# Seven products in place of eight: three more weight pairs of an up projection, with two more buffers and a longer lead

## The chip, the core and the metric

The kernel runs on one core of a Trainium2 chip. The metric is device time in microseconds (us). A core has a matrix engine (PE), whose weight loads are listed apart as PEld; a vector engine (DVE); a scalar engine (ACT); GpSimd (POOL); and SyncE (SP), which here issues most of the DMAs. Each engine works through its own instructions in order and waits on semaphores for the others.

## The reference: what is computed

One decoder layer on 256 tokens of width 2048, in float32: an input projection, two kinds of attention heads, an output projection, a gated MLP and a gate at the end. The change lies in the first product of the MLP, the up projection (`D_FF` is 5632):

```python
h = rms_norm(x, ffn_norm_g[i])
u = h @ w_up[i]                       # (256, 2048) @ (2048, 11264)
a, g = jnp.split(u, 2, axis=-1)
a = causal_dwconv(a, conv_w[i], conv_b[i])
x = x + (jax.nn.gelu(a, approximate=False) * g) @ w_down[i]
```

## The kernel before

**Split numbers.** A float32 product is made of three matrix passes in float32r. Every operand is split into `hi` (the value rounded to float32r) and `lo` (what is left), and a block product is `ah*hi + ah*lo + al*hi` (function `three`, lines 368 to 370). For the weights the split is done on the core, after a load of 512 KB has landed in a "raw" buffer: ACT casts raw to `hi` (line 1308), DVE subtracts `hi` from raw (line 1311). Both halves of a split fill one buffer of 128x1024 each.

**Column groups.** The up projection goes by eleven column groups, `q` = 0 to 10. A group takes 512 columns of `a` and the 512 of `g` that belong to them, for all 256 tokens, and sums over 16 chunks of 128 rows of the weight (k). A plain unit is one k: 2 token halves x 2 column halves = 4 block products, 12 matmuls of 128x512. Its four sums (`up00` to `up11`) fill four of the eight PSUM banks.

**Sevens.** Two k's together make a product of 2x2 blocks by 2x2 blocks, which has eight block products. `seven(r)` does it with seven (the scheme of Strassen and Winograd): sums of weight blocks on DVE, sums of token blocks made beforehand (`S_up`), and seven block products. It is made of four units, which have one, two, two and two block products. They also need one split of 128x512 and three of 128x1024, where two plain units need two of 128x1024, and four additions of 128x512 on DVE (lines 1736 to 1739). Four products (`upP1`, `upP5`, `upP6`, `upP7`) gather over all sevens of a group in the other four PSUM banks. At the last seven of a group they are combined into `z_up` (lines 1765 to 1768), which is added to the group's result afterwards. The table `ORDERS` says for each group where plain units (`p`) and the units of its sevens (`a`, `b`, `c`, `d`) stand. Before the change the groups 0 to 10 have 2, 0, 4, 0, 4, 1, 2, 1, 2, 1 and 1 sevens: 18.

**What else DVE and ACT do for a group.** When the last unit of a group is through, ACT moves the four sums to `EZ` (line 1158, four instructions), and DVE adds `z_up` (line 1165, two instructions) and transposes in blocks (line 205, two). DMAs of POOL and SP turn the result (line 211). Some units later ACT and DVE make the convolution, the GELU, the product with `g` and its split (lines 1184 to 1197, 161, 162), and for the down projection the sums of line 473 to 477. All of this is hooked to fixed units of the next group.

**Lead and buffers.** `run_units` writes the program unit by unit. Before unit `i` it loads as far ahead as raw buffers are free, and splits units up to `i + ahead - 1` as far as split buffers are free. `AHEAD_UP` is 4; in the stretch with four sevens it is 6. There are eight split buffers (`hi0` to `hi3`, `lo0` to `lo3`), and four more (`y0` to `y3`, in the tile `uB`, which is filled with results only later) from the seventh unit of group 1 to the eighth of group 5. Raw buffers are `raw0` to `raw2`, `v4`, and `v0` to `v3`, of which two go two units into group 9 and two go two units into group 10. A seven holds its two raw buffers from its first unit's load to its last unit's split. The order on each engine is then set by a list scheduler when the program is built, so that matmuls of neighbouring units stand mixed on PE.

Of the kernel before, what the change touches and what calls it, by code (L numbers as in the profile page):

```python
# [33 lines left out]

BLK = 1024
RAW, PARTS = 3, 4
AHEAD_UP, AHEAD_FOUR, AHEAD_LATE = 4, 6, 6

SEVEN = (2, 4, 6, 8, 10, 12, 14, 16, 18)
FIRST = (0, 1, 2, 3, 5, 7, 4, 9, 6, 11, 8, 13, 10, 15, 12, 17, 14, 19, 16, 20, 18, 21)  # L40
# [6 lines left out]
UP_K = (4, 5, 6, 7, 0, 1, 2, 3, 8, 9, 10, 11, 12, 13, 14, 15)  # L47
NONE, ONE, TWO = "p" * 16, "pppppp" "apapapap" "pppp", "ppp" "apapapap" "bpbpbpb" "pp"
FOUR = "p" "aapaap" "bbpbb" "ccpccp" "ddpdd" "p"
ORDERS = ("pppppp" "apapapap" "bpbbbp", NONE, FOUR, NONE, FOUR, ONE, TWO, ONE, TWO, ONE, ONE)  # L50
START = [sum(map(len, ORDERS[:q])) for q in range(12)]
TURN_AT = (-1, -1, 0, 0)
GATE_LAST = "ppp" "apapapap" "bbbb" "ppppp"
# [9 lines left out]
def layer_kernel(  # L63
# [29 lines left out]
    def f32(ap):  # L93
        return ap.bitcast(F32)
# [413 lines left out]
    with mixers:  # L508
# [51 lines left out]
        def evac(dst, c0, n, func=AF.Copy):  # L560
            def f(t, b):
                act.activation(dst()[:, t, c0 : c0 + n], b[:, :n], func, scale=r1["t"][:, t : t + 1])
            return f

        def get(name):
            def f():
                if name not in z:
                    z[name] = zbuf(name)
                return z[name]
            return f  # L570
# [320 lines left out]
        def mv_evac(grp):  # L891
            def f(t, b):
                if "mv" not in z:
                    z["mv"] = zbuf("mv")
                    ov = z["mv"].rearrange("p t (h c) -> p t h c", h=MH)[:, :, :, 256:257]
                    pool.memset(ov, 1.0)
                dst = z["mv"][:, t, grp * 516 : (grp + 1) * 516].rearrange("p (h c) -> p h c", h=2)
                act.activation(dst[:, :, 0:256], b.rearrange("p (h c) -> p h c", h=2), AF.Copy,
                               scale=r1["t"][:, t : t + 1])
            return f  # L900
# [38 lines left out]
        def with_after(b, hook):  # L939
            fn = b.fn  # L940
            b.fn = lambda hi, lo: (fn(hi, lo), hook())
# [52 lines left out]
        for c in range(2):  # L994
            f = mv_evac(c)
            add(C_MV + c * 512, 512, after(f, mlstm_out) if c == 1 else f)
        for c in range(2):
            f = evac(get("mo"), c * 512, 512, AF.Sigmoid)
# [96 lines left out]
    with tc.tile_pool(name="ffn", bufs=1) as fp:  # L1095
# [4 lines left out]
        uB = fp.tile([P, 8, 512], F32R, tag="uB", name="uB")  # L1100
        uC = fp.tile([P, 8, 512], F32R, tag="uC", name="uC")
# [58 lines left out]
        def up_turn(with_z):  # L1160

            y = Y.rearrange("p (t b c) -> p t b c", t=NT, b=4)

            def summed(t):
                return lambda: dve.scalar_tensor_tensor(
                    out=EZ[:, t], in0=xs[:, 1, t * BLK : (t + 1) * BLK], scalar=r2["t"][:, t : t + 1], in1=EZ[:, t],
                    op0=ALU.mult, op1=ALU.add)

            def turned(t):
                def f():  # L1170
                    square(y, t, 0, EZ[:, t])
                    if t == NT - 1:
                        with tc.issue_after(last["load"]):
                            move(y, Z, nc.sync)
                return f
            return [f(t) if f is turned or with_z else (lambda: None) for t in range(NT) for f in (summed, turned)]
# [33 lines left out]

        late = {}
        now = [0]
        spaces = [f"raw{i}" for i in range(RAW)] + [f"{k}{i}" for k in ("hi", "lo") for i in range(PARTS)] + ["v0", "v1", "v2", "v3", "v4", "y0", "y1", "y2", "y3"]
        until = {"v0": 8, "v1": 8, "v2": 9, "v3": 9}
        splits = (*spaces[RAW : RAW + 2 * PARTS], "y0", "y1", "y2", "y3", "w0", "w1", "w2", "w3")
        held, used = set(), {}
        for j in range(done[0] - PARTS, done[0]):
            used[f"hi{j % PARTS}"] = used[f"lo{j % PARTS}"] = used[f"raw{j % RAW}"] = len(used)
# [1 line left out]
        def free_spaces(j):  # L1220

            def may(t):
                if t in until:
                    return 7 <= j < START[until[t] + 1] + 2
                if t[0] == "y":
                    return START[1] + 6 <= j < START[5] + 8
                if t == "v4":
                    return j >= 26 and (not late or j < late["x"])
                if t[0] == "x":
                    return j < late["x"]  # L1230
                return (t not in ("pT", "ring") or j < late["gate"]) and (t != "pT" or now[0] > late["x"] - 8) and (t != "pT" or now[0] > late["x"] - 8) and (t not in ("e0", "e1", "ring") or now[0] > late["free"])

            return sorted((t for t in spaces if t not in held and may(t)), key=lambda t: used.get(t, -1))

        def free_of(j, kind):

            return [t for t in free_spaces(j) if (t in splits) == kind]

        def space(j, name, kind):
            tag = free_of(j, kind)[0]  # L1240
            held.add(tag)
            i = int(tag[-1]) if tag[-1].isdigit() else 0
            if tag == "ring":
                v = ring[:, 0:2].rearrange("p a b -> p (a b)")
            elif tag[0] == "e":
                v = EZ[:, i]
            elif tag == "v4":
                v = xs[:, 0, BLK : 2 * BLK]
            elif tag[0] == "y":
                v = f32(uB[:, 2 * i : 2 * i + 2]).rearrange("p k c -> p (k c)")  # L1250
            elif tag[0] == "v":
                v = spare_raws[f"u{32 + 4 * (i // 2)}"][:, i % 2]
            elif tag[0] == "x":
                v = xs[:, 1, i * BLK : (i + 1) * BLK]
            elif tag[0] == "w":
                v = f32(late["w"][:, i]) if i < 4 else late["w2"][:, i - 4]
            elif tag == "pT":
                v = fp.tile([P, BLK], F32R if kind else F32, tag=tag, name=name)
                v = f32(v[:]) if kind else v
            else:  # L1260
                v = wp.tile([P, BLK], F32R if kind else F32, tag=tag, name=name, bufs=1)
                v = f32(v[:]) if kind else v
            return tag, v

        def give(tags):
            for t in tags:
                held.remove(t)
                used[t] = max(used.values(), default=0) + 1
# [48 lines left out]
        def run_units(us, first_late, gate):  # L1317
            loaded = split = 0
            for i, u in enumerate(us):
                if i == first_late:  # L1320
                    v = apool.tile([P, 4, BLK], F32R, tag="aT0", name="w2", bufs=2)
                    S2 = apool.tile([P, 2, BLK], F32R, tag="aT1", name="S2", bufs=2)
                    v2 = apool.tile([P, 2, BLK], F32, tag="aT2", name="w2b", bufs=2)
                    spaces.extend(("w0", "w1", "w2", "w3", "w4", "w5", "pT", "e0", "e1", "ring", "x0", "x1"))
                    late.update(gate=gate, x=i + 20, free=i + 26, w=v, w2=v2, S=S2.rearrange("p b (i c) -> p b i c", c=256))
                ahead = AHEAD_LATE if i >= first_late else AHEAD_FOUR if START[1] + 4 <= i < START[5] else AHEAD_UP
                now[0] = i
                while True:
                    if loaded < len(us) and len(free_of(loaded, False)) >= len(us[loaded].srcs):
                        us[loaded].load(loaded)  # L1330
                        loaded += 1
                    elif split < min(loaded, i + ahead) and len(free_of(split, True)) >= us[split].needs:
                        us[split].split(split)
                        split += 1
                    else:
                        break
                u.fn(*u.parts)
                give(u.holds)
# [350 lines left out]
        def between(hook):  # L1689
            def f():  # L1690
                with tc.issue_after(last["hi"]), tc.issue_after(last["lo"]), tc.issue_after(last["load"]):
                    hook()
            return f
# [5 lines left out]
        def up_group(q):  # L1699
# [3 lines left out]

            n7 = len(set(ORDERS[q]) - {"p"})
            first = 2 * n7
# [83 lines left out]
            kinds = {"p": iter(us), **{c: iter(seven(r)) for r, c in enumerate("abcd"[:n7])}}  # L1789
            return [next(kinds[c]) for c in ORDERS[q]]  # L1790

# [14 lines left out]
        first_late = len(us)  # L1806
# [20 lines left out]
        for q in range(KF // 4):  # L1827
            for job, i in zip(up_turn("a" in ORDERS[q]), TURN_AT if q < KF // 4 - 1 else (-1, 0, -1, 1)):
                with_after(us[START[q + 1] + i], between(job))
            for i, job in enumerate(up_act(q)):  # L1830
                if q < KF // 4 - 1:
                    at = ACT_AT.get(len(ORDERS[q + 1]), ACT_ELSE)
                    with_after(us[START[q + 1] + at[i]], between(job))
# [35 lines left out]
```

## Time and profile before

| what | value |
|---|---|
| median of 3 runs | 1227.51 us (1227.32 to 1229.55) |
| the profiled execution's own time | 1227.41 us |
| its span, first to last instruction | 1225.7 us |
| PE busy | 1219.0 us (99%) |
| DVE busy | 1026.9 us (84%) |
| ACT busy | 765.5 us (62%) |
| POOL busy | 178.7 us (15%) |
| DMA engines, mean busy share by queue | 65.4% and 5.0% for the two large ones |
| granted PE clock | 1.00 |

The busy share of PE is made of matmuls that overlap (one is listed with 0.39 us, while the next starts earlier), so it says that PE always has work, not how long a matmul costs. For that the distance from start to start is read. A wait of an engine is listed with what ended it. The up projection fills the stretch from about 425 us to 898 us of the span.

### The profile page before, as it was taken

The page shows a single profiled execution, that of the slowest core. Times are in us where ns is not written, and L with a number is a line of the kernel's source. Part 1 is how long each engine was busy: PE and PEld are TensorE (multiplying, and loading weights), DVE is VectorE, ACT ScalarE, POOL GpSimd, SP SyncE. Part 2 cuts the span into 40 slices and gives each one's busy share as a digit, 9 for nine tenths or more (in the row PEclk, how much of TensorE's full clock was granted, in tenths as well). Part 3 has the DMA queues.
Part 4 walks back from the last instruction along what each step waited for, and adds up shares of the span by engine and source line. Part 5 has one row for each costly group of instructions (what it writes and reads, how often), then busy time and mean ns, then how long its engine had stood idle before and what let it go on. Part 6 is the DMA issues. An engine that isn't in the chain of part 4 may idle for free.

```text
span 1225.7 us, 16382 instructions
## 1 busy us (share of the span) xinstructions
PE 1219.0 (99%) x5541; PEld 1025.6 (84%) x5541; DVE 1026.9 (84%) x1299; ACT 765.5 (62%) x1119; POOL 178.7 (15%) x331
## 2 busy tenths in 40 slices
PE   9999999999999999999999999999999999999998
PEld 7999988888888888888888888888888888888887
DVE  6788767675679989898898998898788999999796
ACT  8567545565655666776686676767657555556653
POOL 2011237243301401101101100110110000050000
PEclk9999999999999999999999999999999999999999
DMA  8566587676565796767677687756797895785652
GB/s 308 184 193 195 165 241 221 184 216 195 165 234 177 236 292 206 250 215 246 225 264 221 188 267 252 222 175 223 236 315 244 305 359 206 266 252 209 198 200 69
DMA packets 126964, 276.36 MB, mean 225 GB/s; under 512 B 14793, under 2 KB 26817, under 8 KB 126881
## 3 DMA queue, kind: packets, MB, share of 16 engines
q1 hardware_dynamic: 115344, 257.27, 65.4%
q0 software_dynamic: 11008, 17.76, 5.0%
q8 instruction: 43, 0.70, 0.2%
q10 hardware_dynamic: 529, 0.30, 0.1%
q14 instruction: 40, 0.33, 0.1%
HBM read 247.99 MB, written 8.93 MB: 210 GB/s over the span
## 4 chain that ended last, share of the span: by engine, by line
PE 99%; DMA 0%; DVE 0%; SPq 0%; ACT 0%; issue 0%; DVEq 0%
PE up L368 11%; PE up L370 11%; PE up L369 11%; PE tg L357 6%; PE tg L358 6%; PE tg L359 6%; PE pg L368 5%; PE pg L369 5%; PE pg L370 5%; PE gt L370 2%; PE gt L369 2%; PE gt L368 2%; PE upP L368 1%; PE upP L370 1%; PE upP L369 1%; PE dnP L1361 1%
## 5 line engine op out<-in xcount | busy, mean ns | idle before, releaser
L369 PE MATMUL up<-part,x2T 128*128 128x512 f32 x523 | 203.5, 389 | 0.0
L370 PE MATMUL up<-part,x2T 128*128 128x512 f32 x524 | 203.4, 390 | 0.0
L303 DVE TENSOR_TENSOR lo<-raw,hi 128x1024 fp32r<-128x1024 f32 (+3 forms) x119 | 139.2, 1171 | 76.1 <-ACT hi L301 75.7
L1308 ACT CAST part<-raw 128x1024 fp32r<-128x1024 f32 (+1 forms) x139 | 138.7, 1007 | 98.2 <-PE up L370 21.4
L1311 DVE TENSOR_TENSOR part<-raw,part 128x1024 fp32r<-128x1024 f32 (+1 forms) x135 | 155.6, 1162 | 31.6 <-ACT part L1308 27.2
L301 ACT CAST hi<-raw 128x1024 fp32r<-128x1024 f32 (+3 forms) x119 | 120.1, 1011 | 96.3 <-PE tg L359 43.3
L368 PE MATMUL up<-part,x2T 128*128 128x512 f32 x524 | 167.2, 389 | 0.0
L368 PEld LDWEIGHTS up<-part,x2T 128*128 128x128 f32 x524 | 98.4, 188 | 20.3
L369 PEld LDWEIGHTS up<-part,x2T 128*128 128x128 f32 x523 | 98.2, 188 | 20.5
L370 PEld LDWEIGHTS up<-part,x2T 128*128 128x128 f32 x524 | 98.2, 188 | 20.2
L359 PE MATMUL tg<-hi,hT 128*128 128x512 f32 x288 | 113.6, 395 | 0.0
L358 PE MATMUL tg<-lo,hT 128*128 128x512 f32 x288 | 113.3, 393 | 0.0
L357 PE MATMUL tg<-hi,hT 128*128 128x512 f32 x288 | 112.4, 396 | 0.0
L211 POOL DMA_DIRECT2D EZ<-Y x66 | 35.0, 538 | 279.6 <-issue 122.1
L359 PEld LDWEIGHTS tg<-hi,hT 128*128 128x128 f32 x288 | 54.1, 188 | 11.0
L358 PEld LDWEIGHTS tg<-lo,hT 128*128 128x128 f32 x288 | 54.1, 188 | 10.9
L357 PEld LDWEIGHTS tg<-hi,hT 128*128 128x128 f32 x288 | 53.8, 188 | 10.6
L1308 ACT CAST part<-u36r 128x1024 fp32r<-128x1024 f32 x41 | 43.0, 1050 | 21.5 <-PE up L370 15.9
L369 PE MATMUL pg<-lo,hT 128*128 128x430 f32 (+1 forms) x156 | 55.7, 357 | 0.0
L370 PE MATMUL pg<-hi,hT 128*128 128x430 f32 (+1 forms) x156 | 55.5, 356 | 0.0
L1311 DVE TENSOR_TENSOR part<-u36r,part 128x1024 fp32r<-128x1024 f32 x39 | 47.4, 1217 | 6.4 <-ACT part L1308 5.6
L1308 ACT CAST part<-u32r 128x1024 fp32r<-128x1024 f32 (+1 forms) x35 | 34.5, 990 | 24.6 <-PE up L370 8.0
(984 smaller groups left out, 2949.0 us busy)
## 6 DMA issues: line engine op xcount, KB each, us to landing
raw<-in_w_up_dram SPq DMA_DIRECT2D x77, 512.0 KB, 4.9
raw<-in_w_in_dram SPq DMA_DIRECT2D x71, 512.0 KB, 4.4
raw<-in_w_down_dram SPq DMA_DIRECT2D x42, 512.0 KB, 5.5
u36r<-in_w_up_dram SPq DMA_DIRECT2D x41, 512.0 KB, 5.3
u32r<-in_w_up_dram SPq DMA_DIRECT2D x36, 512.0 KB, 5.2
xs<-in_w_up_dram SPq DMA_DIRECT2D x22, 512.0 KB, 5.1
w2b<-in_w_down_dram SPq DMA_DIRECT2D x20, 512.0 KB, 5.6
raw<-in_w_out_dram SPq DMA_DIRECT2D x17, 512.0 KB, 4.8
```

The source lines that it names most:

```text
L211: (other if other and (4 * a + b) % 3 else pool).dma_start(out=c[32 * b : 32 * b + 32, a::4], in_=y[32 * a : 32 * a + 32, :, b])
L301: act.copy(hi, raw)
L303: dve.tensor_sub(lo, raw, f32(hi))
L357: pe.matmul(o, ah, hi[:, i, :], start=first, stop=False)
L358: pe.matmul(o, ah, lo[:, i, :], start=False, stop=False)
L359: pe.matmul(o, al, hi[:, i, :], start=False, stop=last)
L368: pe.matmul(o, ah, hi, start=start, stop=False)
L369: pe.matmul(o, ah, lo, start=False, stop=False)
L370: pe.matmul(o, al, hi, start=False, stop=stop)
L1308: act.copy(r32(hi), raw)
L1311: dve.tensor_sub(r32(lo), raw, hi)
L1361: pe.matmul(o, al, hi, start=False, stop=last)
```

## The change

Groups 5, 7 and 9 get two sevens in place of one, so that groups 5 to 9 have two each, 21 sevens in all. Two split buffers `y4` and `y5` are added in the upper half of the tile `uC`. They may be used from the seventh unit of group 1 to the eighth unit of group 8. While units of groups 5 to 7 are in turn, units up to `i + 4` are split ahead, in place of `i + 3`.

```diff
-AHEAD_UP, AHEAD_FOUR, AHEAD_LATE = 4, 6, 6
+AHEAD_UP, AHEAD_TWO, AHEAD_FOUR, AHEAD_LATE = 4, 5, 6, 6
...
 NONE, ONE, TWO = "p" * 16, "pppppp" "apapapap" "pppp", "ppp" "apapapap" "bpbpbpb" "pp"
 FOUR = "p" "aapaap" "bbpbb" "ccpccp" "ddpdd" "p"
-ORDERS = ("pppppp" "apapapap" "bpbbbp", NONE, FOUR, NONE, FOUR, ONE, TWO, ONE, TWO, ONE, ONE)
+ORDERS = ("pppppp" "apapapap" "bpbbbp", NONE, FOUR, NONE, FOUR, TWO, TWO, TWO, TWO, TWO, ONE)
...
-        spaces = [... "v4", "y0", "y1", "y2", "y3"]
+        spaces = [... "v4", "y0", "y1", "y2", "y3", "y4", "y5"]
...
                 if t[0] == "y":
-                    return START[1] + 6 <= j < START[5] + 8
+                    return START[1] + 6 <= j < START[5 if t < "y4" else 8] + 8
...
-                v = f32(uB[:, 2 * i : 2 * i + 2]).rearrange("p k c -> p (k c)")
+                v = f32(uB[:, 2 * i : 2 * i + 2] if i < 4 else uC[:, 2 * i - 4 : 2 * i - 2]).rearrange("p k c -> p (k c)")
...
-                ahead = AHEAD_LATE if i >= first_late else AHEAD_FOUR if START[1] + 4 <= i < START[5] else AHEAD_UP
+                ahead = AHEAD_LATE if i >= first_late else AHEAD_FOUR if START[1] + 4 <= i < START[5] else AHEAD_TWO if START[5] <= i < START[8] else AHEAD_UP
```

The built program changes in three places that matter for what follows. The first is on DVE, in group 1, where the two new buffers come into use (`part` is a split buffer, the first operand behind the arrow is raw, the second `hi`):

```order
-L1311 TENSOR_TENSOR part_1_4620<-raw_0_4473,part_0_4619 128x1024
+L1311 TENSOR_TENSOR uC<-raw_0_4473,uC 128x1024
 L473 TENSOR_TENSOR Sd_up<-Sd_up 128x2x128
-L1311 TENSOR_TENSOR part_1_4626<-raw_0_4485,part_0_4625 128x1024
-L1311 TENSOR_TENSOR part_1_4642<-u36r,part_0_4641 128x1024
+L1311 TENSOR_TENSOR part_1_4624<-raw_0_4485,part_0_4623 128x1024
+L1311 TENSOR_TENSOR part_1_4640<-u36r,part_0_4639 128x1024
```

The same work stands in the same order there; only its buffers differ.

The second place is on DVE, where group 9 opens. Before, with one seven in that group, which comes later, the stretch around the additions and transposes for group 8 reads:

```order
L1311 TENSOR_TENSOR part_1_7288<-raw_0_7175,part_0_7287 128x1024
L475 TENSOR_TENSOR Sf<-xs,Sf 128x128
L1165 SCALAR_TENSOR_TENSOR EZ<-xs,rstd_ffn,EZ 128x1024 x2
L477 TENSOR_TENSOR Sp<-Sf,Sp 128x4x128
L205 STREAM_TRANSPOSE Y<-EZ 128x8x4x32 x2
L1311 TENSOR_TENSOR part_1_7328<-raw_0_7194,part_0_7327 128x1024
```

Now, with the first seven already in the fourth unit:

```order
L1311 TENSOR_TENSOR part_0_7264<-xs,part_0_7264 128x512
L475 TENSOR_TENSOR Sf<-xs,Sf 128x128
L1165 SCALAR_TENSOR_TENSOR EZ<-xs,rstd_ffn,EZ 128x1024 x2
L1736 TENSOR_TENSOR xs<-xs 128x512
L477 TENSOR_TENSOR Sp<-Sf,Sp 128x4x128
L205 STREAM_TRANSPOSE Y<-EZ 128x8x4x32 x2
L1311 TENSOR_TENSOR part_1_7302<-raw_0_7171,part_0_7301 128x1024
```

What stands ahead of the stretch is now a half split (128x512), and one addition of the seven stands within it.

The third place is the same spot on PE. Before, from the last use of the split ahead of that stretch to the first use of the one behind it:

```order
L369 MATMUL up_7296<-part_1_7288,x2T_3876 128x512
L370 MATMUL up_7296<-part_0_7287,x2T_3876 128x512
L368 MATMUL up_7293<-part_0_7327,x2T_3876 128x512
L368 MATMUL up_7295<-part_0_7327,x2T_3876 128x512
L368 MATMUL up_7294<-part_0_7327,x2T_3876 128x512
L368 MATMUL up_7296<-part_0_7327,x2T_3876 128x512
L368 MATMUL upP_7420<-part_0_7362,x2T_3876 128x512
L369 MATMUL up_7293<-part_1_7328,x2T_3876 128x512
```

Now:

```order
L369 MATMUL upP_7344<-part_0_7264,x2T_3876 128x512
L370 MATMUL upP_7344<-part_0_7264,x2T_3876 128x512
L368 MATMUL up_7270<-part_0_7301,x2T_3876 128x512
L369 MATMUL up_7267<-part_1_7302,x2T_3876 128x512
```

The first use of the low part behind the stretch stood 53 matmuls behind the last matmul of group 8, and stands 43 behind it now. From the middle of group 10 to the end of the program the instructions of PE, DVE and ACT stand in the same order as before.

More of the change, by code (lines that the diff above doesn't have):

```diff
@@ L1212, in layer_kernel @@
         now = [0]
-        spaces = [f"raw{i}" for i in range(RAW)] + [f"{k}{i}" for k in ("hi", "lo") for i in range(PARTS)] + ["v0", "v1", "v2", "v3", "v4", "y0", "y1", "y2", "y3"]
+        spaces = [f"raw{i}" for i in range(RAW)] + [f"{k}{i}" for k in ("hi", "lo") for i in range(PARTS)] + ["v0", "v1", "v2", "v3", "v4", "y0", "y1", "y2", "y3", "y4", "y5"]
         until = {"v0": 8, "v1": 8, "v2": 9, "v3": 9}
-        splits = (*spaces[RAW : RAW + 2 * PARTS], "y0", "y1", "y2", "y3", "w0", "w1", "w2", "w3")
+        splits = (*spaces[RAW : RAW + 2 * PARTS], "y0", "y1", "y2", "y3", "y4", "y5", "w0", "w1", "w2", "w3")
         held, used = set(), {}
```

## The prediction

> **What bounds the kernel now.** I read the page first, then PE's waits, then the stretches of groups 5 to 10.
>
> ```profile
> span 1225.7 us, 16382 instructions
> PE 1219.0 (99%) x5541; PEld 1025.6 (84%) x5541; DVE 1026.9 (84%) x1299; ACT 765.5 (62%) x1119; POOL 178.7 (15%) x331
> PE 99%; DMA 0%; DVE 0%; SPq 0%; ACT 0%; issue 0%; DVEq 0%
> PE warm L111 <- DVE ones L107: 1.1, 1, 1.1
> PE xT L173 <- DMA xs<-in_x_dram: 0.5, 1, 0.5
> ```
>
> The chain that ended last is PE for 99%, and PE's only two waits, the last two rows, are at the program's start. So each matmul taken away shortens the run by one matmul's time, as long as PE still never waits. The price of a matmul is its distance from start to start:
>
> ```profile
> 442.22 0.39 PE L368 MATMUL up<-part,x2T 128*128 128x512 f32 x1
> ...
> 444.94 0.39 PE L369 MATMUL up<-part,x2T 128*128 128x512 f32 x1
> ```
>
> Thirteen starts, twelve steps, 2.72 us: 0.2267 us a step, though each row says 0.39. The other engine near its limit is DVE. Here groups 5 to 10 stand in stretches (us, PE, PEld, DVE, ACT, POOL, granted clock, DMA):
>
> ```profile
> 642.00:682.00 40.00, 40.00 (x178) 33.15 (x177) 34.81 (x37) 24.73 (x36) 3.77 (x7) 1.00 0.73 231
> 682.00:724.00 42.00, 42.00 (x186) 34.68 (x186) 38.80 (x43) 30.65 (x43) 3.75 (x7) 1.00 0.73 230
> 724.00:766.50 42.50, 42.50 (x189) 35.19 (x188) 36.93 (x38) 27.52 (x38) 3.77 (x7) 1.00 0.76 238
> 766.50:809.00 42.50, 42.50 (x189) 35.19 (x188) 39.35 (x44) 30.61 (x42) 3.75 (x7) 1.00 0.66 209
> 809.00:851.50 42.50, 42.50 (x189) 35.19 (x188) 36.83 (x38) 27.51 (x38) 3.77 (x7) 1.00 0.69 216
> 851.50:898.00 46.50, 46.50 (x207) 38.51 (x206) 37.75 (x39) 29.84 (x40) 3.73 (x7) 1.00 0.77 242
> ```
>
> Groups with two sevens (second and fourth row) load DVE with 38.80 and 39.35, those with one (third, fifth) with 36.93 and 36.83. DVE keeps up, but not evenly. Where a group opens it must do the additions and transposes for the group before, and meanwhile makes no weight splits. How near that comes is the lead: the time from the end of a split to PE's first use of its low part. Matching the order of the program with the trace, the opening of group 6 has the smallest:
>
> ```profile
> 694.94 1.22 DVE L1311 TENSOR_TENSOR part<-raw,part 128x1024 fp32r<-128x1024 f32 x1
> 696.33 0.40 PE L369 MATMUL up<-part,x2T 128*128 128x512 f32 x1
> ```
>
> The split ends at 696.16, PE wants it at 696.33: 0.17 us to spare.
>
> **The change, part by part.** *Removed.* A pair of plain units has 8 block products, a seven has 7: 3 matmuls less, for three sevens 9. The built program has 9 fewer. 9 x 0.2267 = 2.04 us.
>
> [...]
>
> *Added.* For each seven ACT and DVE split 3 x 1024 + 512 in place of 2 x 1024 columns, and DVE adds four times.
>
> ```profile
> L1311 DVE TENSOR_TENSOR part<-raw,part 128x1024 fp32r<-128x1024 f32 x38 | 46.2, 1217 | 9.4 <-ACT part L1308 9.2 <-issue 0.2
> L1311 DVE TENSOR_TENSOR part<-u32r,part 128x512 fp32r<-128x512 f32 x3 | 2.1, 686 | 0.4 <-ACT part L1308 0.4
> L1736 DVE TENSOR_TENSOR u32r<-u32r 128x512 f32<-128x512 f32 x3 | 2.0, 672 | 0.0
> L1308 ACT CAST part<-raw 128x1024 fp32r<-128x1024 f32 x37 | 38.8, 1051 | 22.4 <-PE up L370 9.0 <-DVE raw L1737 4.4 <-PE up L369 3.7
> ```
>
> DVE: 1.22 + 0.69 + 4 x 0.67 = 4.6 us a seven; neighbours overlap by about 0.08, so six instructions cost about 4.1. By the stretches a second seven has cost 39.35 - 36.88 = 2.5. A group with two sevens is 186 matmuls on PE, 42.2 us; DVE in it is between the measured 39.35 and 36.88 + 4.1 = 41.0. On average it is hidden behind PE, with 1.2 to 2.8 us to spare in a group. ACT gains some 1.7 us on 27.5: hidden. Loads are the same bytes: nothing on SP or in the DMA queues but their order.
>
> *The openings of groups 6, 7 and 8.* They get one unit more of lead, which on PE is 9 to 12 matmuls, 2.0 to 2.7 us, and two buffers to hold it. From 0.17 that is 2 us and more: no wait, price nothing. Without that cover group 6 would wait for about what its opening adds.
>
> *The opening of group 9.* Here the lead is back at three units and the two buffers are gone, but a second seven has come in. This spot is in the trace, with one seven:
>
> ```profile
> 808.31 2.43 ACT L1158 ACTIVATE EZ<-up,rstd_ffn 128x512 f32<-128x512 f32 x4 [0.53 <-PE up L370]
> 811.81 1.21 DVE L1311 TENSOR_TENSOR part<-raw,part 128x1024 fp32r<-128x1024 f32 x1
> 812.94 0.28 DVE L475 TENSOR_TENSOR Sf<-xs,Sf 128x128 f32<-128x128 f32 x1
> 813.14 2.47 DVE L1165 SCALAR_TENSOR_TENSOR EZ<-xs,rstd_ffn,EZ 128x1024 f32<-128x1024 f32 x2
> 815.53 0.68 DVE L477 TENSOR_TENSOR Sp<-Sf,Sp 128x512 fp32r<-128x512 f32 x1
> 816.14 2.36 DVE L205 STREAM_TRANSPOSE Y<-EZ 128x1024 f32<-128x1024 f32 x2
> 818.43 1.18 DVE L1311 TENSOR_TENSOR part<-raw,part 128x1024 fp32r<-128x1024 f32 x1
> ...
> 821.25 0.39 PE L369 MATMUL up<-part,x2T 128*128 128x512 f32 x1
> ```
>
> The split behind the stretch ends at 819.61, PE uses it at 821.25: 1.64 to spare. In the new order the split ahead is a half one (start to start about 0.60 in place of 1.13) and one addition comes in (about 0.60): the end moves to 819.68. PE's first use moves from 53 to 43 matmuls behind the end of group 8, as the order shows, mostly because a seven's first unit holds PE for 3 matmuls and not 12: 821.25 - 10 x 0.2267 = 818.98. So the split is late by 0.70 us, and PE waits so long. What is queued behind that matmul is all of group 9, so the wait goes to the end in full, once; DVE is then ahead again.
>
> Bounds of this wait. Below: nothing, if ACT and DVE come 0.7 earlier (ACT waits for PE's last sums in the first row above). Above: the half split that opened group 8,
>
> ```profile
> 769.69 0.68 DVE L1311 TENSOR_TENSOR part<-raw,part 128x512 fp32r<-128x512 f32 x1
> 775.47 0.39 PE L369 MATMUL upP<-part,x2T 128*128 128x512 f32 x1
> ```
>
> had a lead of 5.10; with the stretch of 7.25 on DVE (0.20 + 2.39 + 0.61 + 2.29 from the starts above, 0.60 for the addition, 1.16 for the split) and 3 matmuls on PE, 5.10 + 0.68 - 7.25 = -1.47. I take 0.70, from the rows of the spot itself.
>
> *Sum.* -2.04 + 0.70 = -1.34 us. The profiled execution took 1227.41 and would take 1226.07; the median of the runs is 0.10 above it, so 1226.2. The gain is 0.11%; a measurement of this kernel can tell about 0.2% (2.46 us) from no change, and the full 2.04 us would also stay below that.
>
> **The rivals.** *No wait at all.* Group 9 opens in time and the whole 2.04 is kept: 1225.5. For it: PE has not waited once at eleven openings, and the scheduler mixes matmuls of several units. Against it: 0.17 and 1.64 us are little room.
>
> *DVE becomes the bound, slower.* DVE waits too:
>
> ```profile
> DVE part L1311 <- ACT part L1308: 18.9, 21, 2.1
> ACT part L1308 <- PE up L370: 32.1, 25, 5.7
> ```
>
> That is 18.9 us in the 220 us of groups 5 to 9, 3.7 a group. If these waits stay while the work grows, groups 5, 7 and 9 need 41.0 + 3.7 = 44.7 on DVE against 42.2 on PE, 2.5 us too much each. The first of it is taken from the room at the openings (1.64 and the 2.0 to 2.7 of the new unit, about 4), the rest PE waits: 3 x 2.5 - 4 = 3.5, and 1227.51 - 2.04 + 3.5 = 1229.0. It decides from the point where a group costs DVE over 42.2 with its waits. Against it: the second row says that ACT itself waits for PE to free a buffer, so these waits are slack, and more buffers shorten them.
>
> *Late loads.* In group 10, with few raw buffers, ACT waited for a load:
>
> ```profile
> 874.84 2.00 ACT L1308 CAST part<-raw 128x1024 fp32r<-128x1024 f32 x2 [4.27 <-DMA raw<-in_w_up_dram]
> ```
>
> PE did not. Group 9 now has a second seven that holds two of the six raw buffers left. A wait of this size on the lead of 1.64 would cost 2.6: 1226.2 + 2.6 = 1228.8. Against it: counting units in the program, loads there still stand 7 or more units ahead of use, over 14 us.
>
> [...]
>
> **How the numbers follow.** The forecast with a wait of 0.3 to 1.5 us has 0.50 (1225.8 to 1227.0), no wait 0.25, DVE as the bound 0.14, late loads 0.08, something else 0.03. Range: 1225.2, a little under the full gain, to 1228.2, which takes in the mild part of the two slow rivals: about 0.8. Faster by over 0.2%, under 1225.05, needs more than the matmuls give: 0.08. Slower by over 0.2%, above 1229.96, is the bad part of the slow rivals: 0.07. The rest, 0.85, is within 0.2%.
>
> **What would show it.** In the profile after: 9 matmuls fewer (some records may be missing); in groups 5 to 9 steps of 0.2267 with no gap except one of about 0.7 us at the fourth unit of group 9, where PE waits for DVE's line 1311; DVE at 39 to 41 us in each of these groups; leads at the openings of groups 6 to 8 of 2 us or more. Gaps at several openings, or DVE idle for ACT as much as before while PE waits, would make the prediction wrong, as would a load that PE's wait goes back to.

## The result, and the profile after

The changed kernel takes 1244.47 us (median; 1242.42 to 1246.9). Beside it the kernel before took 1227.51 again. The ratio is 1.0136, with a 95% interval of 1.0124 to 1.0147: slower by 17 us, where 1226.2 was forecast with a range up to 1228.2. The profiled execution of the changed kernel is the longest of its five (1246.9).

The page of the changed kernel, with the lines that answer to those of before:

```profile
span 1245.2 us, 16395 instructions
PE 1224.9 (98%) x5532; PEld 1026.8 (82%) x5532; DVE 1039.2 (83%) x1317; ACT 769.8 (62%) x1125; POOL 179.2 (14%) x331
PE 95%; DMA 1%; DVE 1%; SPq 1%; ACT 1%; issue 0%; DVEq 0%; ACTq 0%
```

PE's waits (us in total, times, the longest):

```profile
PE up L368 <- ACT part L1308: 8.3, 2, 6.7
PE upP L368 <- ACT uC L1308: 2.2, 1, 2.2
PE xT L173 <- DMA xs<-in_x_dram: 2.2, 1, 2.2
...
PE up L369 <- DVE part L1311: 1.0, 2, 0.6
```

PE has its 9 matmuls less, and it now waits: the first, second and last row are new. Where, and what the clock did there, the stretches show (us, PE, PEld, DVE, ACT, POOL, granted clock, DMA):

```profile
700.00:704.00 4.00, 3.50 (x8) 2.75 (x9) 4.00 (x5) 1.39 (x2) 0.71 (x2) 0.57 0.88 278
704.00:823.00 119.00, 119.00 (x526) 98.54 (x525) 110.52 (x120) 84.00 (x115) 8.12 (x15) 1.00 0.71 227
823.00:825.50 2.50, 1.91 (x9) 1.25 (x8) 2.50 (x4) 1.10 (x2) 1.46 (x3) 1.00 0.59 218
825.50:838.00 12.50, 12.50 (x57) 10.33 (x56) 10.12 (x11) 4.84 (x5) 1.74 (x4) 1.00 0.75 218
838.00:853.00 15.00, 12.96 (x53) 9.29 (x52) 8.44 (x9) 12.56 (x21) 0.00 (x0) 1.00 0.61 195
853.00:872.00 19.00, 19.00 (x85) 15.68 (x85) 19.00 (x21) 11.26 (x14) 0.00 (x0) 1.00 0.57 171
872.00:892.00 20.00, 13.00 (x43) 9.59 (x42) 11.24 (x13) 6.30 (x8) 3.74 (x7) 0.74 0.54 159
892.00:914.00 22.00, 22.00 (x99) 18.22 (x98) 16.72 (x16) 15.47 (x24) 0.00 (x0) 1.00 0.85 286
```

Now count, at every start of a matmul, by how much it comes later than 0.2267 us after the one before. Four places lose: the opening of group 6 2.69 us, and 1.40 by steps at half rate; the opening of group 9 0.86; the middle of group 9 3.07; the opening of group 10 8.07, and 2.60 at half rate. That is 18.7 us, less 2.04 for the matmuls 16.7. From the first matmul of the up projection to PE's last end the changed kernel needs 17.0 more than before. The rest of the run differs only at the program's start, by up to 2.7 us from run to run (part of it is the third wait above, 0.5 before), in kernels that do the same there. So the experiments are compared by the stretch from the first matmul of the up projection to PE's last end, 795.97 us before. The expectations go by a shorter one, to the first matmul of the down projection: 470.24 us before and 487.25 after.

The largest loss, on SP, ACT and PE (start, time, engine; in brackets the idle time before):

```profile
863.01 2.61 SPq L1281 DMA_DIRECT2D raw<-in_w_up_dram  x2
872.47 7.27 SPq L211 DMA_DIRECT2D EZ<-Y  x10
879.85 0.60 SPq L1281 DMA_DIRECT2D raw<-in_w_up_dram  x1
...
878.88 0.59 ACT L1765 COPY xs<-upP 128x512 f32<-128x512 f32 x1 [6.00 <-PE upP L370]
884.43 1.99 ACT L1308 CAST part<-raw 128x1024 fp32r<-128x1024 f32 x2 [4.97 <-DMA raw<-in_w_up_dram]
...
878.45 0.39 PE L370 MATMUL upP<-part,x2T 128*128 128x512 f32 x1
885.53 2.07 PE L368 MATMUL up<-part,x2T 128*128 128x512 f32 x4 [6.69 <-ACT part L1308]
887.40 0.63 PE L369 MATMUL up<-part,x2T 128*128 128x512 f32 x1
887.83 0.63 PE L370 MATMUL up<-part,x2T 128*128 128x512 f32 x1
```

The load of group 10's eighth unit (the seventh in the expectations, which count from 0) is issued at 879.85, right behind the ten DMA issues of the turn, which hold SP for 7.3 us. It lands at 884.41, ACT casts it, PE goes on 7 us late, and then at half rate (0.43 us a step; the granted clock from 881.50 to 891.70 is 0.50). The same place before:

```profile
861.20 0.54 SPq L1281 DMA_DIRECT2D xs<-in_w_up_dram  x1
862.35 7.26 SPq L211 DMA_DIRECT2D EZ<-Y  x10
869.71 0.60 SPq L1281 DMA_DIRECT2D raw<-in_w_up_dram  x1
```

There the ten are as long, but they begin 10 us after PE's first use of group 10 (852.08; after: 16 us, 856.26), and stand behind 10 loads of the group. In the changed program they stand behind 8. For group 9 it is 9 in place of 10.

### The profile page after: what moved, and what is told of

It is laid out like the page before. It is cut to its first block, busy times and chain, and to the rows that moved or that the text cites. A ratio compares the mean times of both kernels' runs of the same rounds, so it can differ in the third digit from the quotient of the medians.

```text
span 1245.2 us, 16395 instructions
## 1 busy us (share of the span) xinstructions
PE 1224.9 (98%) x5532; PEld 1026.8 (82%) x5532; DVE 1039.2 (83%) x1317; ACT 769.8 (62%) x1125; POOL 179.2 (14%) x331
## 4 chain that ended last, share of the span: by engine, by line
PE 95%; DMA 1%; DVE 1%; SPq 1%; ACT 1%; issue 0%; DVEq 0%; ACTq 0%
PE up L369 10%; PE up L370 10%; PE up L368 10%; PE tg L357 6%; PE tg L358 6%; PE tg L359 6%; PE pg L368 5%; PE pg L369 5%; PE pg L370 4%; PE gt L370 2%; PE gt L369 2%; PE gt L368 2%; PE upP L368 1%; PE upP L370 1%; PE upP L369 1%; PE dnP L1359 1%
## 5 line engine op out<-in xcount | busy, mean ns | idle before, releaser
L1308 ACT CAST part<-raw 128x1024 fp32r<-128x1024 f32 (+1 forms) x130 | 128.4, 997 | 94.8 <-PE up L370 26.4
L369 PE MATMUL up<-part,x2T 128*128 128x512 f32 x452 | 178.4, 395 | 1.2 <-DVE part L1311 1.0
L370 PE MATMUL up<-part,x2T 128*128 128x512 f32 x450 | 176.4, 394 | 0.0
L1311 DVE TENSOR_TENSOR part<-raw,part 128x1024 fp32r<-128x1024 f32 (+1 forms) x124 | 141.3, 1149 | 33.6 <-ACT part L1308 27.4
L368 PE MATMUL up<-part,x2T 128*128 128x512 f32 x450 | 148.9, 393 | 8.3 <-ACT part L1308 8.3
L368 PEld LDWEIGHTS up<-part,x2T 128*128 128x128 f32 x450 | 84.8, 189 | 27.1 <-ACT part L1308 9.4
L369 PEld LDWEIGHTS up<-part,x2T 128*128 128x128 f32 x452 | 86.1, 191 | 20.9 <-DVE part L1311 2.8
L370 PEld LDWEIGHTS up<-part,x2T 128*128 128x128 f32 x450 | 85.5, 190 | 17.6
L357 PEld LDWEIGHTS tg<-hi,hT 128*128 128x128 f32 x288 | 54.2, 189 | 10.7
L1308 ACT CAST part<-u36r 128x1024 fp32r<-128x1024 f32 (+1 forms) x40 | 40.9, 1029 | 21.8 <-PE up L370 7.8
L1311 DVE TENSOR_TENSOR part<-u36r,part 128x1024 fp32r<-128x1024 f32 (+1 forms) x37 | 44.0, 1190 | 10.7 <-ACT part L1308 10.2
```

The source lines that it names most:

```text
L357: pe.matmul(o, ah, hi[:, i, :], start=first, stop=False)
L368: pe.matmul(o, ah, hi, start=start, stop=False)
L369: pe.matmul(o, ah, lo, start=False, stop=False)
L370: pe.matmul(o, al, hi, start=False, stop=stop)
L1308: act.copy(r32(hi), raw)
L1311: dve.tensor_sub(r32(lo), raw, hi)
```

## The experiments

In the expectations, **Q** says that the ten issues on SP make weight loads late; **D** that DVE and ACT have too little time at the openings; **C** that the loss of group 10 follows from that of group 9; **R** that raw buffers are short, so that loads go late; **B** and **B2** that the order or the number of the buffers for split weights is at fault at group 6. "After" is the changed kernel. The table has what PE loses at each place (gaps and steps at half rate, us) and what PE needs from the up projection on, against before (orders_alone also loses 1.0 in group 5). Each row is one profiled execution. Where group 6 opens, the gap is 2.4 us in six rows; the 4.0 and 4.1 among them have steps at half rate behind it and the 2.5 have not, and this does not come from the edits (see the last section).

| run | group 6 opens | 7 | 8 | 9 opens | 9, middle | 10 opens | against before |
|---|---|---|---|---|---|---|---|
| before | 0 | 0 | 0 | 0 | 0 | 0 | 0 |
| after | 4.1 | 0 | 0 | 0.9 | 3.1 | 10.7 | +17.0 |
| buffers_alone | 0 | 0 | 0 | 0 | 0 | 0 | 0.0 |
| sevens_5_7 | 2.5 | 0.2 | 0.7 | 0 | 0 | 0 | +2.1 |
| seven_9 | 0 | 0 | 0 | 1.2 | 2.4 | 7.4 | +10.7 |
| orders_alone | 2.1 | 1.5 | 2.2 | 0.6 | 4.5 | 9.2 | +19.1 |
| turn8_on_pool | 2.5 | 0.1 | 1.2 | 0.9 | 2.5 | 10.3 | +15.8 |
| turns8_9_on_pool | 4.0 | 0 | 0 | 0.9 | 2.6 | 2.7 | +8.5 |
| turns_later | 4.1 | 0 | 0 | 0.9 | 3.5 | 3.5 | +10.3 |
| raws_longer | 2.5 | 0 | 0.6 | 0.9 | 0 | 0 | +2.0 |
| buffers_g6 | 0.9 | 0.9 | 1.7 | 0.9 | 2.6 | 10.4 | +15.8 |
| both_buffers | 0.9 | 1.3 | 1.7 | 0.9 | 0 | 0 | +2.9 |

### Which part of the change loses what

The buffers and the lead without the new orders:

```diff
-ORDERS = (..., FOUR, TWO, TWO, TWO, TWO, TWO, ONE)
+ORDERS = (..., FOUR, ONE, TWO, ONE, TWO, ONE, ONE)
```

> Edit: the two buffers and the lead of five units are kept, the orders of the groups are those of before (18 sevens). After took 1244.47 us against 1227.51, and its trace shows PE short of work in three places: the opening of group 6 (about 4 us with the steps at half rate), the middle of group 9 (3), the opening of group 10 (11). Theory Q (SP's queue): groups 9 and 10 lose because the ten DMA issues of the turn stand on SP ahead of weight loads that are then late; here the ten stand behind 10 loads of groups 9 and 10, as before, so nothing is lost there. Theory D (DVE and ACT short of time): without the three sevens nothing is lost anywhere; both say 1227.5, within 1. Theory B (the longer lead and the buffers change the order of casts for the worse by themselves): the opening of group 6 loses its 4 us here too: 1231.

Measured: 1228.52 us, ratio 1.0002 (0.9992 to 1.0012). No gap at all: B falls as a cause by itself. The next two have the buffers and a part of the sevens, the third all sevens and neither buffers nor lead:

```diff
-ORDERS = (..., FOUR, TWO, TWO, TWO, TWO, TWO, ONE)
+ORDERS = (..., FOUR, TWO, TWO, TWO, TWO, ONE, ONE)   # sevens_5_7
+ORDERS = (..., FOUR, ONE, TWO, ONE, TWO, TWO, ONE)   # seven_9
```

> Edit: as after, but group 9 has one seven as before: 20 sevens, 6 matmuls less than before, 1.36 us. On SP the ten issues of the turn stand behind 10 loads of groups 9 and 10 as before. Theory Q: groups 9 and 10 lose nothing, the opening of group 6 still loses about 4: 1227.5 - 1.4 + 4 = 1230. Theory D with a debt that adds up from group to group (five groups with two sevens): group 9 and 10 still lose something, since DVE gets only one of the three relieved: 1233 or more. If group 6's loss hung on group 9's order too: 1226.

> Edit: as after, but groups 5 and 7 have one seven as before: 19 sevens, 3 matmuls less, 0.68 us. The ten issues of the turn stand behind 9 loads of group 9 and 9 of group 10, where before had 10 and 10 and after 9 and 8. Theory Q: the first 0.7 us wait at the opening of group 9 comes, and the loads behind the ten issues are late in the middle of group 9 (3 us) and, one load better off than after, by less at the opening of group 10 (2 to 8, half rate included): 1227.5 - 0.7 + 0.7 + 3 + 2 to 8 = 1233 to 1239. Theory D with an adding debt: groups 5 to 8 are relieved, so group 9 loses its 0.7 and little else: 1228.

> Edit: the new orders (21 sevens), without the two buffers and with four units of lead everywhere. On SP the ten issues stand behind 10 loads of group 9 and 8 of group 10. My prediction's step said that the buffers are what keeps the openings of groups 6 to 8 free of waits: then each of the three loses here about what its opening adds, 1 to 2 us and more with steps at half rate, groups 9 and 10 as after: 1247 to 1252. Theory B (lead and buffers cost at group 6): the 4 us there vanish: about 1240. Theory Q: with 10 loads ahead in group 9 its middle loses nothing, the opening of group 10 loses its 11 us.

Measured: sevens_5_7 1230.06 us, ratio 1.0022 (1.0012 to 1.0031); seven_9 1237.97, 1.0081 (1.0064 to 1.0098); orders_alone 1248.76, 1.0163 (1.0148 to 1.0178). The first two lie where Q put them, the third in the range that the prediction's own step gave (the buffers as cover). The losses belong mostly to their own sevens: those of groups 5 and 7 cost at the openings of groups 6 and 8 and nothing in groups 9 and 10, and that of group 9 alone makes 11.0 of the 14.6 us that groups 9 and 10 lose in after. So a debt that adds up from group to group is not what costs most there; the other 3.6 us come only with all three. Q has one miss: in orders_alone the ten issues stand behind 10 loads of group 9, and its middle loses 4.5 us all the same. So the place of the ten on SP is not the whole cause.

### The ten issues on SP

```diff
-for job, i in zip(up_turn("a" in ORDERS[q]), ...):
+for job, i in zip(up_turn("a" in ORDERS[q], None if q in (8, 9) else nc.sync), ...):
...
-move(y, Z, nc.sync)
+move(y, Z, q_)
```

(turns8_9_on_pool; `None` leaves all sixteen DMAs of a turn to POOL. turn8_on_pool has only `q == 8`. In turns_later the call of `move` becomes a job of its own, four units further on, for q in (8, 9).)

> Edit: as after, but the sixteen DMAs of the turn of the ninth group (which run while group 9 opens) are all issued by POOL, none by SP; the turn of group 9 stays as it is. From the first matmul of the up projection to the first of the down projection before needs 470.2 us, after 487.3. In after the middle of group 9 loses 3.1 us, the opening of group 10 10.7 (6.9 of it one wait, 2.6 half rate). Theory Q (each block of ten issues delays the loads behind it): the middle of group 9 loses nothing, the opening of group 10 goes on losing most of its 10.7, the up projection takes 484. Theory C (a cascade: the late loads of group 9 hold up ACT and DVE, so DVE comes 6 us late to the transposes of group 10, the ten issues start late, and so on): both go, 487.3 - 3.1 - 9 = 475. Theory D (DVE simply has too much work): 487.

> Edit: as after, but the DMAs of the turns that run while groups 9 and 10 open are all issued by POOL, none by SP. Theories Q and C: weight loads of groups 9 and 10 are issued when their buffer comes free, so the middle of group 9 loses nothing; at the opening of group 10 the load of the seventh unit, issued at 879.85 in after, would go when DVE has split the unit whose buffer it takes, 6 us sooner, and the wait of 6.9 us shrinks to 1 or less, half rate included: the up projection takes 474 to 476 in place of 487.3, the run 1231 to 1234. Theory D (DVE too busy at the openings): little changes, 485 to 487. POOL takes 16 x 0.53 = 8.5 us for a turn in place of 3.2; if ACT waits for the turned columns, a loss of some us appears at ACT's lines 1184 and 1187.

> Edit: as after, but the DMAs of the turns that run while groups 9 and 10 open are placed four units later in the program: on SP the ten issues stand behind 11 loads of the group in place of 9 and 8 (before: 10 and 10). Nothing else is moved by hand. Theory Q: what matters is how many weight loads stand ahead of the ten issues: with 11 the losses of groups 9 and 10 go but for a rest of 2 or so, the up projection takes 474 to 477. Theory D: 486 to 488. A rival within Q: the loads behind the ten are late all the same, only later in the group, and ACT's lines 1184 and 1187 wait for columns that now come later: 480 or more.

Measured: turn8_on_pool 1243.32 us, ratio 1.0128 (1.0113 to 1.0143); turns8_9_on_pool 1237.07, 1.0077 (1.006 to 1.0094); turns_later 1237.73, 1.0084 (1.0069 to 1.0099). Taking the ten off SP, or putting them behind 11 loads, takes 8 and 7 of group 10's 10.7 us away. In turns8_9_on_pool the ninth load of group 10, the one that PE's long wait went back to, is issued 8.5 us behind the eighth (870.80), in after 14.8. So Q is right there. It does next to nothing for the middle of group 9 (3.1 to 2.6, or 3.5), and so all three miss Q's forecasts of the up projection: 486.0 where 484 was expected, 478.7 where at most 476 and 478.6 where at most 477. In the middle of group 9 the load that ACT waits for is late without any turn on SP. In turns8_9_on_pool:

```profile
822.84 0.54 SPq L1281 DMA_DIRECT2D raw<-in_w_up_dram  x1
827.12 0.54 SPq L1281 DMA_DIRECT2D u36r<-in_w_up_dram  x1
828.25 0.54 SPq L1281 DMA_DIRECT2D xs<-in_w_up_dram  x1
829.39 0.88 SPq L1281 DMA_DIRECT2D raw<-in_w_up_dram  x1
...
837.55 1.04 ACT L1308 CAST part<-raw 128x1024 fp32r<-128x1024 f32 x1 [5.61 <-DMA raw<-in_w_up_dram]
```

SP is free between these loads and waits for raw buffers: from 812 to 842 seven of its waits, 16.4 us, end with DVE's line 1311, the last to read a raw buffer of a plain unit. What the DMA engines do meanwhile, from 812 to 832 in slices of 0.5 us (busy tenths, GB/s):

```profile
DMA  1000009598100000049910568759999999599998
GB/s 62 0 0 0 0 4 119 164 389 324 49 0 0 0 0 0 0 172 410 418 49 0 131 131 78 90 180 418 426 275 205 230 201 143 115 348 393 344 283 336
```

They are idle for 5.5 of the first 8.5 us. Then four loads are issued between 827.12 and 830.52, and the third of them, issued at 829.39, lands at 837.53, after 8.1 us where the median of such loads on the changed kernel's page is 5.1. C cannot be read from turn8_on_pool, since group 9 hardly got better in it.

### Raw buffers

The changed kernel lets v0 and v1 go at the second unit of group 9, v2 and v3 at that of group 10. The tiles they lie in are written again only late in those groups, so they can be kept:

```diff
-return 7 <= j < START[until[t] + 1] + 2
+return 7 <= j < START[until[t] + 1] + 12
```

> Edit: as after, but the raw buffers v0, v1 (v2, v3) are used ten units longer, to START[9] + 12 (START[10] + 12) in place of + 2, so groups 9 and 10 have two raw buffers more in their first half. The ten issues of the turn then stand behind 11 and 10 loads of groups 9 and 10 (after: 9 and 8, before: 10 and 10). With both turns on POOL the middle of group 9 still lost 2.6 of its 3.1 us: the queues of the DMAs were empty for some 7 us there, the load of the second half of the second seven waited for its raw buffer till 827.12 and the next ones followed in a bunch. Theory R (too few raw buffers, so loads go late, and the ten issues make them later): group 9 keeps its 0.75 at the opening and loses its 3.1, group 10 its 10.7 but for 2: the up projection takes 487.25 - 3.1 - 8.7 = 475.5. Theory Q alone (only the place of the ten issues counts): group 10 gets better by 8, the middle of group 9 by no more than 0.5: 478.7.

Measured: 1230.39 us, ratio 1.0022 (1.0013 to 1.0032). The 13.7 us in the middle of group 9 and at the opening of group 10 are gone, all of them, with the turn's ten issues still on SP. The up projection takes 472.3, less than R's 475.5: group 10 keeps no rest, and the gap at group 6 brings no half rate here. The waits of PE:

```profile
PE upP L368 <- ACT uC L1308: 2.2, 1, 2.2
...
PE up L369 <- DVE part L1311: 0.6, 1, 0.6
PE upP L368 <- ACT part L1308: 0.3, 1, 0.3
```

And SP where group 10 opens:

```profile
859.60 0.54 SPq L1281 DMA_DIRECT2D raw<-in_w_up_dram  x1
865.07 6.60 SPq L211 DMA_DIRECT2D EZ<-Y  x10
871.77 0.60 SPq L1281 DMA_DIRECT2D xs<-in_w_up_dram  x1
```

None of PE's waits goes back to a load any more, and the ten begin 12.0 us after PE's first use of group 10 (853.03) in place of 16. They also stand behind 11 loads of group 9 and 10 of group 10 now, so this edit moves what Q is about as well. So R holds, with Q as its second half. It fits C too that DVE comes to group 10's transposes 4 us sooner after that first use, but no run took group 9's loss away alone, so C stays open.

### The openings that are left

> Edit: as after, with two more buffers for split weights (four more than before), the lower half of uC, allowed from START[5] to START[7] + 8, and six units of lead in groups 5 and 6 in place of five. Groups 9 and 10 are untouched. In after the opening of group 6 loses 4.1 us (a wait of 2.4 for the first half split of its first seven, and 1.4 of half rate); ahead of it ACT stands still for 5.4 us since its next cast waits for a buffer that PE has not given back. Theory B2 (the buffers are what is short there): the 4 us go, the up projection takes 483. Theory D (the sums, additions and transposes of the opening keep DVE too long): the wait stays or shrinks by less than 1: 486 to 487.

> Edit: as after, with two more buffers for split weights (the lower half of uC), now allowed only from START[5] + 8 to START[7] + 8, after the last sum that lies there has been used, and the lead left at five. In the run with four more buffers they were taken from START[5] on, so that the last sevens of the fifth group read overwritten sums, and the lead was six; the opening of group 6 lost nothing there, but the middle and the end of it 9 us. Theory B2 (at the opening of group 6 it is buffers that are short): the 4.1 us go here too, and nothing comes in elsewhere, 483. Rival (the longer lead removed the wait there, not the buffers): no change, 487.

> Edit: the two edits together, raw buffers ten units longer and two more buffers for split weights. If the four places found are all, only the wait of 0.75 us at the opening of group 9 and a rest of 2 at that of group 10 stay: the up projection takes 470.24 - 2.04 + 2.8 = 471.0, the run about 1228, the same as before. If R is right and group 10 keeps nothing: 469.0, the run 1226.3. If the losses only move, 475 and more.

> Edit: as both_buffers, and the DMAs of the turns that run while groups 9 and 10 open all issued by POOL. What the ten issues on SP still cost then shows as the difference between the two: nothing if the loads already stand far enough ahead (469 to 471 both), 1 to 2 us less here if group 10's loads are still late behind them.

Measured: four_more_buffers 1248.61 us, ratio 1.0173 (1.0158 to 1.0188); buffers_g6 1243.3, 1.0128 (1.0114 to 1.0141); both_buffers 1230.41, 1.0022 (1.0013 to 1.003); both_buffers_pool 1231.51, 1.003 (1.0018 to 1.0042). With two buffers more from START[5] + 8 on,

```diff
-"y0", "y1", "y2", "y3", "y4", "y5"
+"y0", "y1", "y2", "y3", "y4", "y5", "y6", "y7"
...
+if t in ("y6", "y7"):
+    return START[5] + 8 <= j < START[7] + 8
```

the gap at group 6 shrinks from 2.4 to 0.8 us, and groups 7 and 8 lose more. The four openings together lose 4.0 in raws_longer and 4.8 in both_buffers: the loss moved. The forecasts of buffers_g6 and both_buffers missed (486.1, between 483 and 487; 473.1, between 471 and 475). four_more_buffers, with a lead of six and the buffers from START[5] on, opened group 6 in time (0.2), and then lost 9 us at the end of it and in group 7. In it the two buffers lie on sums that the last sevens of the group before still read, so it does not compute the layer, and only its times are used here. Turns on POOL bring nothing once the raw buffers suffice: both_buffers_pool loses the same at the openings of groups 6 to 9 as both_buffers to within 0.1 us, and 0.5 more in group 10.

The gap at group 6 is a wait for the fourth unit of its first seven. (The expectations call it a first half split; the row shows a full one, 128x1024, behind the seven's last addition.) Why that split is late, in the changed kernel:

```profile
693.77 1.06 ACT L1308 CAST part<-u32r 128x1024 fp32r<-128x1024 f32 x1 [5.43 <-PE up L369]
696.62 0.61 ACT L476 CAST Sp<-Sf 128x512 fp32r<-128x512 f32 x1
699.40 1.04 ACT L1308 CAST uC<-raw 128x1024 fp32r<-128x1024 f32 x1 [2.16 <-DVE raw L1739]
...
697.27 0.69 DVE L477 TENSOR_TENSOR Sp<-Sf,Sp 128x512 fp32r<-128x512 f32 x1 [0.89 <-ACT Sp L476]
697.88 0.68 DVE L1738 TENSOR_TENSOR raw<-raw,u36r 128x512 f32<-128x512 f32 x1
698.60 0.69 DVE L1739 TENSOR_TENSOR raw<-raw 128x512 f32<-128x512 f32 x1
...
700.50 0.73 PE L368 MATMUL upP<-uC,S_up 128*128 128x512 f32 x1 [2.23 <-ACT uC L1308]
```

ACT stands still for 5.43 us until a matmul of PE's line 369 is through; as the expectations read it, its next cast needs the buffer that PE then gives back. So ACT's small cast of line 476 comes late, DVE waits for it in turn, the additions 1738 and 1739 stand behind it, then ACT waits for these, and PE for ACT. Line 476's result is only stored for the down projection. The last four runs put it and its neighbours (lines 473 to 477) on POOL:

```diff
-def sums_of(u, f, t):
+def sums_of(u, f, t, dve=dve):
...
-    act.copy(t[:, :, 0:P], f)
+    (act.copy if dve is nc.vector else dve.tensor_copy)(t[:, :, 0:P], f)
...
-    sums_of(u, f, t)     # in left_sums
+    sums_of(u, f, t, pool)
```

> Edit: as raws_longer, and the five instructions of left_sums (lines 473 to 477, 1.65 us of DVE and 0.6 of ACT at each opening) run on POOL. raws_longer's up projection took 472.26 us: 470.24 - 2.04 and 4.0 of waits at the openings of groups 6 (2.5), 8 (0.6) and 9 (0.9). Theory D (DVE and ACT short of time at the openings): the waits shrink by up to 1.65 each, 0.9 stays: 469.1, the run 1226.4. Theory B (order and number of the split buffers): the waits stay, 472. A rival: POOL is slower at this and shares something with DVE, DVE's rows get longer and the waits grow: 474.

> Edit: as both_buffers (raw buffers longer, two more buffers for split weights), and the sums of left_sums on POOL. both_buffers lost 0.9, 1.3, 1.7 and 0.9 at the openings of groups 6 to 9, its up projection took 473.09. Theory D: each of the four shrinks by up to 1.65, nothing or 0.1 stays: 468.3 to 468.6, the run 1225.7, faster than before. Theory B: 472 to 473.

> Edit: as after, and the sums of left_sums on POOL. Theory D for the openings with raw buffers as the cause of the rest: the openings of groups 6 and 9 lose 2.5 to 3.5 us less than after, the middle of group 9 and the opening of group 10 as after: 487.25 - 3 = 484. If DVE's lateness is what makes the ten issues of group 10 come late: DVE comes 1.65 us sooner, group 10 loses 1.65 less as well: 482. Theory B: 487.

> Edit: the kernel before (18 sevens), with the sums of left_sums on POOL. PE never waits there, so all theories say 470.24 for the up projection and 1227.5 for the run, unless POOL's work makes DVE slower by more than the leads of 0.2 us at group 6 hold: then 471 or more.

Measured: 1230.63 us, ratio 1.0024 (1.0015 to 1.0034); 1230.51, 1.0022 (1.0012 to 1.0033); 1243.5, 1.0133 (1.0117 to 1.0148); and 1227.78, 1.0005 (0.9996 to 1.0014) for the kernel before. At the openings of groups 6 to 9 PE loses 1.9, 1.5, 0.8 and 1.0 in raws_longer_sums_pool (5.3 in place of 4.0), 0.4, 1.0, 2.2 and 1.0 in both_buffers_sums_pool (4.7 in place of 4.8), 0.9, 1.7, 1.3 and 1.1 in after_sums_pool. In the last the middle of group 9 and the opening of group 10 still lose 3.9 and 7.8. Even the kernel before now waits, 0.4 us at the opening of group 8. So the wait at group 6 shrinks each time and others grow; the sum stays between 4.0 and 5.3 us in these kernels and in after. Neither this move nor more buffers removes it. The up projections take 473.6 (the rival with longer rows of DVE said 474), 473.0 (B: 472 to 473), 485.3 (between D and B) and 470.6, so none of D's forecasts for the first three came true. D is not refuted by this, as the move gives DVE less than the 1.65 us an opening that were counted on. Its splits get longer beside POOL's work: of the 112 splits of 128x1024 from 640 to 900 in raws_longer_sums_pool, 16 take over 1.26 us, and 14 of these overlap one of the moved instructions (the first row is raws_longer, the next two raws_longer_sums_pool, from 640 to 900):

```profile
L1311 DVE TENSOR_TENSOR part<-raw,part 128x1024 fp32r<-128x1024 f32 (+1 forms) x39 | 45.7, 1179 | 5.3 <-ACT part L1308 4.7 <-PE up L370 0.4
```

```profile
L1311 DVE TENSOR_TENSOR part<-raw,part 128x1024 fp32r<-128x1024 f32 (+1 forms) x39 | 49.0, 1262 | 7.2 <-ACT part L1308 7.2
L477 POOL TENSOR_TENSOR Sp<-Sf,Sp 128x512 fp32r<-128x512 f32 x7 | 12.7, 1816 | 0.6
```

What sets the sum at the openings stays open. The chain above is one path of it. Every edit also gave PE, ACT and DVE a new order, and that the next path then took over is a reading that no run tested. No kernel tried is faster than the one before: what is left of the change after its large losses are mended is 2.04 us of matmuls against 4 us of waits.

## Why the prediction was wrong, step by step

**Right.** The matmuls: 9 fewer at 0.2267 us. The wait at the opening of group 9: forecast 0.70 us, at PE's line 369 for DVE's line 1311, for the split behind the transposes. Measured 0.75 in the gap, with 0.59 of it as a wait of that pair:

```profile
823.94 0.39 PE L368 MATMUL up<-part,x2T 128*128 128x512 f32 x1
824.91 0.50 PE L369 MATMUL up<-part,x2T 128*128 128x512 f32 x1 [0.59 <-DVE part L1311]
```

Also right: no wait at the openings of groups 7 and 8 in the changed kernel (smallest leads 1.6 and 1.2 us, where 2 and more was forecast), and that the buffers and the lead are the cover there: orders_alone lost 1.5 and 2.2 without them.

**The step that failed first: "Loads are the same bytes: nothing on SP or in the DMA queues but their order."** The order was the price. A seven takes two raw buffers for its first unit and gives them back with its fourth, so with two sevens and six raw buffers (four once v2 and v3 are gone) the loads of group 9's second half and of group 10 are issued late and in bunches, and behind the turn's ten issues. It cost 13.7 of the 18.7 us lost; raws_longer, where these are gone, shows it.

**The rival of late loads was the right mechanism and had the wrong size.** It had a chance of 0.08 and a price of 2.6 us, worked from one ACT wait of 4.27. What kept it low was the count of 7 units and 14 us between load and use. That counts units in the program's own order, where a load is written as soon as `run_units` counts a buffer as free. In the traces the load waits on SP until the buffer's last split is done (from 640 to 895 in the changed kernel 49 of SP's waits, 96.2 us, end with DVE's line 1311), and behind what stands ahead of it. In the changed kernel the load of group 9's thirteenth unit is issued at 833.13, and PE asks for it 6.8 us later:

```profile
833.13 0.54 SPq L1281 DMA_DIRECT2D raw<-in_w_up_dram  x1
...
840.44 1.04 ACT L1308 CAST part<-raw 128x1024 fp32r<-128x1024 f32 x1 [4.42 <-DMA raw<-in_w_up_dram]
...
841.54 1.20 PE L368 MATMUL up<-part,x2T 128*128 128x512 f32 x4 [1.59 <-ACT part L1308]
```

The 4.27 itself was the warning: in the kernel before, that load (869.71 above) was already right behind the ten issues, and all that kept PE from waiting was its lead there.

**"They get one unit more of lead ... no wait" failed at group 6** (2.7 us of gap and 1.4 of half rate). The step counted the lead in matmuls of PE and left out that ACT's casts wait for PE, 5.43 us there. The new buffers and the longer lead brought nothing at this opening: orders_alone lost 2.1 us at it without them. Two buffers more cut the gap to 0.8, but groups 7 and 8 then lost more, so what bounds the openings stays open.

**DVE as the bound** had a price of 3.5 us by adding up groups. The sum of the openings' waits, 4.0 to 5.3, is near it, but it did not shrink when sums were taken off DVE, so that mechanism is not shown, and the nearness may be chance.

**The clock** has no term in the forecast's sum; it is 1.00 in all six stretches of before. In the changed kernel steps at half rate lost 4.0 us, behind waits of 2.2 and 6.7 us.

## What to carry to other kernels

When a change makes some units hold their input buffers longer, count the buffers through the stretch and date each load by when its buffer comes free on the engine that frees it, not by its place in the program. Then look at what stands ahead of that load on the issuing queue: ten small DMA issues took 7 us here, more than the load's own 4.6. A gain of a few matmuls is worth what the tightest opening leaves of it, and there each added seven, worth 0.68 us, cost 0.6 to 2.5 even in raws_longer.

## What the runs showed of the hardware

Half rate came after a short wait, but not always. The gap at group 6's opening was 2.4 us over a step in six of the runs (a wait of 2.23 in the changed kernel). In the changed kernel, turns8_9_on_pool and turns_later 7 steps of 0.43 us followed it, in sevens_5_7, raws_longer and turn8_on_pool none.

In these traces it goes by where the gap falls. In each trace the granted clock changes only at times that lie a whole number of 3.413 us apart (in turn8_on_pool 255 of them at full clock from the start of the run on, then three at half). Laid over the traces, these windows hold the whole gap where half rate followed, and cut it in two where it did not: 1.93 + 0.46 us in raws_longer, 1.25 + 1.15 in sevens_5_7, 1.16 + 1.23 in turn8_on_pool. Here are two neighbouring windows of the changed kernel and, below, of raws_longer (columns as above; 3.41 us each):

```profile
697.18:700.59 3.41, 1.18 (x6) 0.66 (x4) 3.29 (x5) 1.25 (x3) 3.40 (x7) 1.00 0.65 158
700.59:704.01 3.42, 3.42 (x8) 2.65 (x9) 3.42 (x4) 0.80 (x1) 0.12 (x1) 0.50 0.88 280
```

```profile
694.93:698.34 3.41, 1.64 (x8) 1.02 (x6) 2.73 (x4) 1.25 (x3) 3.07 (x6) 1.00 0.50 112
698.34:701.75 3.41, 2.95 (x13) 2.44 (x14) 3.41 (x4) 1.87 (x3) 0.67 (x2) 1.00 0.93 299
```

The eighteen traces have 2621 such windows at full clock between the up projection's first matmul and 930 us. In each, add up what PE's steps of over 0.26 us take beyond 0.2267. All 14 windows that lose 2.15 us or more are followed by one at half rate, and none of those that lose 2.03 or less is. So in these runs the same gap of 2.4 us cost 1.4 us more, or nothing, by the chance of its place. Half rate then held on for 3 to 6 us of work (in the changed kernel from 700.59 to 704.01 at group 6, and from 885.53 to 891.74 at group 10).

One DMA issue of the turn took about 0.7 us on SP (ten in 6.6 to 7.3 in the rows above) and 0.53 on POOL (six in 3.19, in the changed kernel).
